# Seven block products in place of eight in the second layer of a two-layer decoder trunk

## The chip, the cores and the metric

The kernel runs on one core of one Trainium2 chip, in one launch. The metric is the device time of a run in microseconds (us); the host only lays arrays out before and after. Three runs of the kernel before took 833.39, 834.37 and 834.68 us.

## What is computed

One inference step of a trunk of two layers, over 512 prompt positions and 8 sample positions that share all parameters: 520 positions of 1024 channels, in float32. The first layer (two convolutions behind an input projection of 7168 columns, then an output projection) is computed as before. The second layer is:

```python
def c_mixer(x, w_in, w_s, b_s, norm_v_g, norm_v_b, w_out):
    z = jnp.einsum('bld,de->ble', x, w_in)             # 1024 -> 3 x 2048
    u, v, g = jnp.split(z, (D_C, 2 * D_C), axis=-1)
    u = jax.nn.gelu(u)
    v = layer_norm(jax.nn.gelu(v), norm_v_g, norm_v_b)  # over all 2048 channels
    ...
    w_causal = w_s * jnp.tril(jnp.ones((CHUNK, CHUNK), w_s.dtype))
    mix = jnp.einsum('hts,bnshd->bnthd', w_causal, vc) + jnp.transpose(b_s)[None, None, :, :, None]
    mix = mix.reshape(bsz, n_chunks * CHUNK, D_C)[:, :seq]
    y = u * mix * jax.nn.silu(g)
    return jnp.einsum('ble,ed->bld', y, w_out), v
```

`vc` is v in chunks of 128 positions and 8 groups of 256 channels. Each layer ends in `x = layer_norm(alpha * x + mixer(x))`.

## The kernel before

**Layout.** Channels lie on the 128 partitions, the 520 positions along the free axis in two halves of 260 (`TH`), since one half fits a bank of PSUM. A product is exact to float32 by splitting both sides into a high and a low part in the type fp32r: per slice of 128 input channels and per half, three matmuls, high by high, low by high, high by low. A **unit** is 128 output channels of 1024 inputs: 8 slices x 2 halves x 3 = 48 matmuls of 260 columns. `mm2` (L154 to L168) issues a unit with both halves side by side, `mm` (L142) one half; `zt` takes a z tile of two banks from the PSUM pool `zps`, which has two such buffers, `cps` has two single banks, `mps` two for transposes and mixes.

**Weights.** `load_unit` (L116) takes a unit's 512 KB from DRAM on SyncE's DMA queue (`raw`, three buffers), has ScalarE cast the high part (`whi`, L121), and VectorE subtract the low part (`wlo`, L128); for units 10 to 49 ScalarE writes the negated weight (L125) and GpSimd's queue adds the weight onto it by an accumulating DMA (L126). Twelve slots hold high and low parts; `unit(n)` keeps five units loaded ahead.

**Order.** The engines run in order. The order on each is fixed when the program is built, by a scheduler that walks the code with a model of time and with the priorities that `soon()` (earlier) and `background()` (later) set.

**Second layer.** x1 is the first layer's result (`res`), split into `x1h` and `x1l`.

1. Sixteen v units. The first six go by halves (L630 to L641), ten by `mm2` (L642 to L647). Each gets a gelu on ScalarE and then `v_tok` (L616): four transposes on TensorE to put positions on the partitions, a copy out by ScalarE (L622) into `vtok`, four statistics on VectorE (L624). All sixteen `vtok` stay in SBUF.
2. `v_finish` (L655): mean and variance per position, and 64 normalisations of 128x128 on VectorE (L663), in place; also the row sums of w_s and the samples' part.
3. `c_group(g0)` (L733), four times. Each does four u units with a gelu (L741), then the four gate units with a silu (L756); for each gate VectorE forms u·gate (L757), `mix_unit` (L710) does four mixing matmuls with `vtok` (L718), and `split_y` (L400) multiplies by the mix and splits y into high (ScalarE, L406) and low (VectorE). Gelu and silu need different function tables on ScalarE: a table load stands where one follows the other, so twice a group.
4. After two groups, eight output units `z_q` (L773) over the first 1024 channels of y, put into `r1`; after the other two, `out_part` (L482), the second half of the output projection with the final norm.

Of the kernel before, what the change touches and what calls it, by code (L numbers as in the profile page):

```python
# [20 lines left out]
NS = 8  # L21
# [20 lines left out]

LEAD = 5
CUT = 260
NWARM = 28
POOL_MUL = (3, 7)
# [4 lines left out]
def decoder_kernel(  # L51
# [45 lines left out]
    def zt(name):  # L97
        return zps.tile([P, 2, 512], F32, tag="z", name=name)
# [13 lines left out]

    n_units = 2 + wu.shape[0]
    units = [None, None]

    def load_unit(wtag=("W", 12)):  # L116
        n = len(units)
        raw = wpool.tile([P, KT, P], F32, tag="raw", name=f"raw_{n}", bufs=3)
        nc.sync.dma_start(raw, wu[n - 2])
        hi = wpool.tile([P, KT, P], F32R, tag=wtag[0], name=f"whi_{n}", bufs=wtag[1])  # L120
        nc.scalar.copy(hi, raw)  # L121
        lo = wpool.tile([P, KT, P], F32R, tag=wtag[0], name=f"wlo_{n}", bufs=wtag[1])
        if n in BY_DMA:

            nc.scalar.mul(lo, raw, -1.0)  # L125
            nc.gpsimd.dma_start(lo, wu[n - 2], accum_op=ALU.add)  # L126
        else:
            nc.vector.tensor_tensor(lo, raw, hi.bitcast(F32), op=ALU.subtract)  # L128
# [12 lines left out]

# [146 lines left out]
    for i in range(KT):  # L288
# [70 lines left out]
    with background():  # L359
        for j in range(2):  # L360
            nc.gpsimd.dma_start(cas_out[:, 4 * j : 4 * j + 4], xs[j])
            proda = wpool.tile([P, 4, NS, WA], F32, tag="M", name=f"proda_{j}", bufs=4)
            nc.vector.tensor_tensor(
                proda,
                xs[j],
                pa[:, 4 * j : 4 * j + 4, None, PA_W : PA_W + WA].to_broadcast([P, 4, NS, WA]),
                op=ALU.mult,
            )
            cas = tiny.tile([P, 4, NS], F32, name=f"cas_{j}")
            nc.vector.tensor_reduce(cas, proda, axis=AX.X, op=ALU.add)  # L370
            for i in range(4 * j, 4 * j + 4):
                nc.scalar.activation(
                    cA[i][:, SEQ:], cas[:, i - 4 * j, :], AF.Identity, bias=pa[:, i, PA_B : PA_B + 1]
                )
# [83 lines left out]
    for d in range(KT):  # L458
        xr = tmp(f"xr_{d}")
        nc.sync.dma_start(xr, xT[:, d, :])  # L460
        r = slots.tile([P, T], F32, tag="SB", name=f"r_{d}", bufs=8)
# [12 lines left out]
        res.append(r)  # L474
# [138 lines left out]
    vs = tiny.tile([P, NV, NS], F32, name="vs")  # L613
    stats = wpool.tile([P, NC, NV, 6], F32, tag="M", name="stats", bufs=4)

    def v_tok(i):  # L616
        nc.gpsimd.tensor_copy(vs[:, i, :], vt[i][:, SEQ:])
        m = mt(f"vt_{i}")
        for c in range(NC):
            nc.tensor.transpose(m[:, c * P : (c + 1) * P], vt[i][:, c * P : (c + 1) * P], ident)  # L620
        t = ab_slot(f"vtok_{i}") if i < 8 else slots.tile([P, T], F32, tag="SB", name=f"vtok_{i}", bufs=8)
        nc.scalar.copy(t[:, :SEQ], m)  # L622
        for c in range(NC):
            nc.vector.bn_stats(stats[:, c, i, :], t[:, c * P : (c + 1) * P])  # L624
        vtok[i] = t

# [6 lines left out]
    for i in range(NVF):  # L633
# [6 lines left out]
        if i > 0:  # L640
            v_tok(i - 1)  # L641
    for i in range(NVF, NV):  # L642
        z = zt(f"z_v{i}")
        mm2(halves(z), unit(n + i), x1h, x1l)
        vt[i] = y_slot(F32, f"v_{i}")
        nc.scalar.activation(two(vt[i]), zh(z), AF.Gelu_apprx_tanh)
        v_tok(i - 1)  # L647
    n += NV

    mv = tiny.tile([P, NC, 2], F32, name="mv")  # L650
    rs = tiny.tile([P, NC], F32, name="rs")
    mixs = tiny.tile([P, NV, NS], F32, name="mixs")
    rowsum = wpool.tile([P, NH, P], F32, tag="M", name="rowsum", bufs=4)

    def v_finish():  # L655
        v_tok(NV - 1)
# [3 lines left out]
        nc.gpsimd.tensor_tensor(rs, rs, neg_half[:, :NC], op=ALU.pow)  # L660
        for i in range(NV):
            for c in range(NC):
                nc.vector.tensor_scalar(  # L663
                    vtok[i][:, c * P : (c + 1) * P],
                    vtok[i][:, c * P : (c + 1) * P],
                    mv[:, c, 0:1],
                    rs[:, c : c + 1],
                    op0=ALU.subtract,
                    op1=ALU.mult,
                )  # L670

# [37 lines left out]

    def mix_unit(i):  # L710
        h = i // 2
# [5 lines left out]
        for c in range(NC):  # L717
            nc.tensor.matmul(  # L718
                m[:, c * P : (c + 1) * P], vtok[i][:, c * P : (c + 1) * P], wt[:, h, :], start=True, stop=True
            )  # L720
# [11 lines left out]

    def c_group(g0):  # L733
        nonlocal n
        gu = []
        for i in range(g0, g0 + 4):
            z = zt(f"z_u{i}")
            mm2(halves(z), unit(n), x1h, x1l)
            n += 1
            t = btmp(f"gu_{i}")  # L740
            nc.scalar.activation(two(t), zh(z), AF.Gelu_apprx_tanh)  # L741
            gu.append(t)
            if i == 0:
                v_finish()

        def finish(i):
            t = gu[i - g0]
            split_y(i, t, mix_unit(i), "c", 1)

        for i in range(g0, g0 + 4):  # L750
            z = zt(f"z_gc{i}")
            mm2(halves(z), unit(n), x1h, x1l)
            n += 1
            g = tmp(f"silu_c{i}")
            t = gu[i - g0]
            nc.scalar.activation(two(g), zh(z), AF.Silu)  # L756
            nc.vector.tensor_tensor(t, g, t, op=ALU.mult)  # L757
            if g0 > 0:
                finish(i)
        if g0 == 0:  # L760
            for i in range(4):
                finish(i)
# [129 lines left out]
```

## Time and profile before

| | us |
|---|---|
| median of three runs | 834.37 |
| profiled execution, time | 834.73 |
| profiled execution, span from the first to the last instruction | 833.0 |
| mean granted TensorE clock, share of full | 0.990 |
| VectorE, ScalarE, GpSimd busy (share of the span) | 536.6 (64%), 347.2 (42%), 88.0 (11%) |
| share of the DMA queues of SyncE and GpSimd of 16 engines | 32.2%, 15.0% |

PE is TensorE's matmuls and PEld its weight loads, DVE is VectorE, ACT ScalarE, POOL GpSimd, SP SyncE; a q behind a name is that engine's instruction queue. A group row gives line, engine, operation, output <- inputs with shape and type, xcount, then busy time in us and mean ns of one, then the engine's idle time just before these instructions with what ended most of it. A row of the chain of waits gives start, duration, engine and work, in us. A row of windows gives the stretch in us, then seven or more entries in the order PE, PEld, DVE, ACT, POOL: the busy time with the count of instructions, then the mean granted clock, the DMA share and GB/s.

### The profile page before, as it was taken

Reading aid. Unit: us, or ns where it says so; the run is one execution under the profiler, and the core shown is the slowest. Engines: PE = TensorE matmul, PEld = TensorE weight load, DVE = VectorE, ACT = ScalarE, POOL = GpSimd, SP = SyncE. Lnnn points to the kernel's source line nnn. Section 1 sums busy time; section 2 is a strip of 40 time slices with the busy share of each in tenths; the row PEclk is TensorE's granted clock in tenths of the full one; section 3 lists DMA queues with packets and bytes.
Section 4 is the critical chain, followed back from the end, with each engine's and each line's share of the span. In section 5 each row is a group of like instructions: output and inputs, shape, how many; then the busy total and the mean of one; then the engine's idle time right before and its main releaser. Section 6 shows DMA issues by size and latency. Waiting matters only on the chain.

```text
span 833.0 us, 16028 instructions
## 1 busy us (share of the span) xinstructions
PE 814.2 (98%) x6792; PEld 812.2 (98%) x6792; DVE 536.6 (64%) x914; ACT 347.2 (42%) x510; POOL 88.0 (11%) x158
## 2 busy tenths in 40 slices
PE   8999999999999999999989999999999999999994
PEld 8999999999999999999979999999999999999993
DVE  5899998999962576446885432596355433526566
ACT  5545454455354444442647423323432133334243
POOL 0121221221110000000021111100000000000032
PEclk9999999999999999999989999999999999999997
DMA  8798988889888543231331432214233223222011
GB/s 290 208 206 191 209 185 185 184 191 216 182 173 189 167 115 102 79 124 52 84 119 51 128 85 93 77 56 126 78 87 92 84 94 102 77 87 92 1 53 52
DMA packets 32873, 103.37 MB, mean 124 GB/s; under 512 B 4209, under 2 KB 7937, under 8 KB 32801
## 3 DMA queue, kind: packets, MB, share of 16 engines
q1 hardware_dynamic: 26000, 79.01, 32.2%
q0 software_dynamic: 6800, 23.33, 15.0%
q8 instruction: 53, 0.87, 0.4%
q14 instruction: 20, 0.16, 0.1%
HBM read 98.89 MB, written 3.44 MB: 123 GB/s over the span
## 4 chain that ended last, share of the span: by engine, by line
PE 96%; DMA 1%; DVE 1%; ACT 0%; SPq 0%; issue 0%; ACTq 0%; DVEq 0%
PE z_p L146 11%; PE z_gc L162 11%; PE z_u L162 11%; PE z_v L162 7%; PE z_q L162 6%; PE z_o L162 6%; PE z_c L162 5%; PE z_ga L162 5%; PE z_post L162 5%; PE z_h L162 5%; PE z_gb L162 5%; PE z_val L162 5%; PE z_gate L162 5%; PE z_v L146 5%; PE mix L718 2%; PE vt L620 1%
## 5 line engine op out<-in xcount | busy, mean ns | idle before, releaser
L121 ACT CAST whi<-raw 128x1024 fp32r<-128x1024 f32 x134 | 139.9, 1048 | 324.9 <-PE z_u L162 44.9
L128 DVE TENSOR_TENSOR wlo<-raw,whi 128x1024 fp32r<-128x1024 f32 x94 | 114.4, 1224 | 142.5 <-ACT whi L121 141.9
L274 DVE SCALAR_TENSOR_TENSOR acc<-apad,pa,acc 128x512 f32<-128x512 f32 x240 | 165.7, 751 | 3.6 <-ACT acc L271 2.7
L162 PE MATMUL z_gc<-x1h,whi 128*128 128x260 f32 x256 | 72.9, 285 | 0.0
L162 PE MATMUL z_u<-x1h,whi 128*128 128x260 f32 x256 | 72.4, 283 | 0.0
L162 PE MATMUL z_gc<-x1h,wlo 128*128 128x260 f32 x256 | 72.0, 281 | 0.0
L162 PE MATMUL z_u<-x1l,whi 128*128 128x260 f32 x256 | 72.0, 281 | 0.0
L162 PE MATMUL z_gc<-x1l,whi 128*128 128x260 f32 x256 | 72.0, 281 | 0.0
L162 PE MATMUL z_u<-x1h,wlo 128*128 128x260 f32 x256 | 72.0, 281 | 0.0
L126 POOL DMA_DIRECT2D wlo<-in_wu x40 | 34.7, 869 | 139.2 <-ACT wlo L125 132.2
L162 PEld LDWEIGHTS z_u<-x1h,wlo 128*128 128x128 f32 x256 | 48.1, 188 | 0.1
L162 PEld LDWEIGHTS z_gc<-x1h,wlo 128*128 128x128 f32 x256 | 48.2, 188 | 0.0
L162 PEld LDWEIGHTS z_gc<-x1l,whi 128*128 128x128 f32 x256 | 48.1, 188 | 0.0
L162 PEld LDWEIGHTS z_u<-x1h,whi 128*128 128x128 f32 x256 | 48.0, 188 | 0.1
L162 PEld LDWEIGHTS z_u<-x1l,whi 128*128 128x128 f32 x256 | 48.1, 188 | 0.0
L162 PEld LDWEIGHTS z_gc<-x1h,whi 128*128 128x128 f32 x256 | 48.1, 188 | 0.0
L162 PE MATMUL z_v<-x1h,whi 128*128 128x260 f32 x160 | 46.0, 287 | 0.0
L162 PE MATMUL z_v<-x1h,wlo 128*128 128x260 f32 x160 | 45.0, 281 | 0.0
L162 PE MATMUL z_v<-x1l,whi 128*128 128x260 f32 x160 | 45.0, 281 | 0.0
L125 ACT ACTIVATE wlo<-raw 128x1024 fp32r<-128x1024 f32 x40 | 42.2, 1055 | 0.0
L162 PE MATMUL z_c<-xh,wlo 128*128 128x260 f32 x128 | 36.1, 282 | 0.3 <-DVE wlo L128 0.3
L146 PE MATMUL z_p<-yh_c,whi 128*128 128x260 f32 x128 | 36.3, 284 | 0.0
(260 smaller groups left out, 2723.4 us busy)
## 6 DMA issues: line engine op xcount, KB each, us to landing
raw<-in_wu SPq DMA_DIRECT2D x134, 512.0 KB, 3.9
wlo<-in_wu POOLq DMA_DIRECT2D x40, 512.0 KB, 7.7
xr<-in_xT SPq DMA_DIRECT2D x8, 260.0 KB, 4.2
x<-in_xT SPq DMA_DIRECT2D x7, 260.0 KB, 5.1
out_y<-r SPq DMA_DIRECT2D x8, 130.0 KB, 1.7
out_y<-out SPq DMA_DIRECT2D x4, 260.0 KB, 2.2
raw_s<-in_w SPq DMA_DIRECT2D x8, 128.0 KB, 4.5
xs<-in_cache_a SPq DMA_DIRECT2D x2, 496.0 KB, 8.2
```

Of the source, the lines that this page charges most:

```text
L121: nc.scalar.copy(hi, raw)
L125: nc.scalar.mul(lo, raw, -1.0)
L126: nc.gpsimd.dma_start(lo, wu[n - 2], accum_op=ALU.add)
L128: nc.vector.tensor_tensor(lo, raw, hi.bitcast(F32), op=ALU.subtract)
L146: nc.tensor.matmul(ps, a[:, k, :], b[k][:, c], start=(k == 0 and j == 0), stop=(k == KT - 1 and j == 2),)
L162: nc.tensor.matmul(z[h][:, :TH], a[:, k, :], b[k][:, hs(h)], start=(k == 0 and j == 0), stop=(k == KT - 1 and j == 2),)
L274: nc.vector.scalar_tensor_tensor(acc[i], apads[i][:, j : j + SEQ], pa[:, i, PA_W + j : PA_W + j + 1], acc[i], op0=ALU.mult, op1=ALU.add,)
L620: nc.tensor.transpose(m[:, c * P : (c + 1) * P], vt[i][:, c * P : (c + 1) * P], ident)
L718: nc.tensor.matmul(m[:, c * P : (c + 1) * P], vtok[i][:, c * P : (c + 1) * P], wt[:, h, :], start=True, stop=True)
```

## The change

**Block products.** Two units with the same inputs, (W1, W2), are taken as a 2x2 matrix of blocks: two units by two halves of 512 input channels; x1 likewise: two halves of the channels by two halves of the positions. Such a product of 2x2 blocks can be had with seven products of blocks in place of eight. One product is 4 slices x 3 = 12 matmuls of 260 columns; a pair takes 84 where two units take 96. Pairs are ten v units (6 to 15, five pairs) and twelve of the sixteen (u unit, gate unit) **items**; items 3, 7, 11 and 15 (`PLAIN`) stay two units each.

**What that needs.** Sums of weight blocks (`load_pair`): four sums on VectorE (s1 to s4, 128x512), five high parts on ScalarE (`ws1` to `ws4`, `wa22`, L153) and five low parts on VectorE, beside high and low of W1. Sums of x1's blocks, once (`x_forms`): 16 sums on VectorE, 16 high parts and 16 low parts. Sums of the results (`Seven`): a z tile and one bank of `cps` collect them, three copies out by ScalarE and three additions by VectorE with a PSUM operand.

**What it moves.** An item now runs through at once, so that its gelu (L910) and its two silu (L911 reads PSUM, L912 the SBUF half) stand together, after the *next* item's first product (`step`); weights are asked for by jobs, ten slots ahead (`need`). v goes to DRAM from `v_tok`, and comes back for one item at a time (`fetch`) on SyncE's queue; its normalisation, four activations with scale and bias (L869), is ScalarE's. `r1` goes to DRAM and back as well. In the second layer W1's low part of a pair, and both of a plain item, come by the accumulating DMA.

```diff
-LEAD = 5
+WSLOTS = 12
+AHEAD = 10
+PLAIN = (3, 7, 11, 15)
...
+    def load_pair(n1, n2):
+        r1 = load_raw(n1)
+        hi, lo = parts(n1, r1)
+        r2 = load_raw(n2)
...
+        def split(h, low, src):
+            nc.scalar.copy(h, src)
+            nc.vector.tensor_tensor(low, src, h.bitcast(F32), op=ALU.subtract)
...
+        a11, a12, a21, a22 = r1[:, :4], r1[:, 4:], r2[:, :4], r2[:, 4:]
+        s1 = add("s1", a21, a22)
+        s2 = add("s2", s1[2], a11)
+        split(*s1)
+        s4 = add("s4", s2[2], a12)
+        split(*s2)
+        s3 = add("s3", a11, a21)
+        split(*s3)
+        split(*form("a22"), a22)
+        split(*s4)
...
+    def need(*job):
+        j = place[job]
+        ahead = lambda: sum(2 if len(q) == 1 else 7 for q in JOBS[j + 1 : len(loaded)])
+        while len(loaded) < len(JOBS) and (len(loaded) <= j or ahead() < AHEAD):
...
-        t = ab_slot(f"vtok_{i}") if i < 8 else slots.tile([P, T], F32, tag="SB", name=f"vtok_{i}", bufs=8)
-        nc.scalar.copy(t[:, :SEQ], m)
+        t = tmp(f"vtok_{i}")[:, :SEQ]
+        nc.scalar.copy(t, m)
         for c in range(NC):
             nc.vector.bn_stats(stats[:, c, i, :], t[:, c * P : (c + 1) * P])
-        vtok[i] = t
+        vtok[i] = spill.tile([P, SEQ], F32, name=f"vd_{i}")
+        nc.gpsimd.dma_start(vtok[i], t)
...
+        def head(self):
+            (hi, lo), self.w = need(*self.job)
...
+            product(self.b1, self.a1(0), self.x(0, 0), True)
+            with soon():
+                nc.scalar.copy(self.s12[:, hs(0)], self.b1)
+
+        def body(self):
+            product(self.b2, self.s("s1"), self.f(1), True)
+            product(self.b1, self.s("s2"), self.f(2))
+            with soon():
+                nc.scalar.copy(self.s12[:, hs(1)], self.b1)
+            b3 = cps.tile([P, SEQ], F32, tag="cv", name=f"z_{self.key}_2")[:, :TH]
+            product(b3, self.a1(1), self.x(1, 0), True)
+            with soon():
+                nc.vector.tensor_tensor(self.c1[:, hs(0)], self.s12[:, hs(0)], b3, op=ALU.add)
+            product(self.b1, self.s("s3"), self.f(3))
+            with soon():
+                nc.scalar.copy(self.s3, self.b1)
+                nc.vector.tensor_tensor(self.c22, self.s3, self.b2, op=ALU.add)
+
+        def tail(self):
+            product(self.b1, self.s("a22"), self.f(4))
+            product(self.b2, self.s("s4"), self.x(1, 1))
+            with soon():
+                nc.vector.tensor_tensor(
+                    self.c1[:, hs(1)], self.s12[:, hs(1)], self.b2, op=ALU.add
+                )
+            return self.b1
...
+    def step(p, end):
+        p.head()
+        if flight[0] is not None:
+            flight[0]()
+        p.body()
+        flight[0] = end
...
-        for i in range(NV):
-            for c in range(NC):
-                nc.vector.tensor_scalar(
...
+        nc.vector.scalar_tensor_tensor(nmr, mv[:, :, 0], -1.0, rs, op0=ALU.mult, op1=ALU.mult)
...
+    def fetch(i):
+        t = tmp(f"vback_{i}")[:, :SEQ]
+        nc.sync.dma_start(t, vtok[i])
+        for c in range(NC):
+            nc.scalar.activation(
...
+    def gate_end(p, i, g):
+        z = p.tail()
+        nc.scalar.activation(p.c1, p.c1, AF.Gelu_apprx_tanh)
+        nc.scalar.activation(g[:, hs(0)], z, AF.Silu, scale=-1.0)
+        nc.scalar.activation(g[:, hs(1)], p.c22, AF.Silu, scale=-1.0)
+        finish(i, p.c1, g)
...
+        t = spill.tile([P, T], F32, name=f"rd_{d}")
+        nc.gpsimd.dma_start(t, r)
...
+        r = r_slot(f"r2_{d}")
+        nc.sync.dma_start(r, r1[d])
```

**Order on ScalarE, items 8 to 10.** Before, the gate part of the third group, from the table load at its first silu:

```order
L756 ACT_TABLE_LOAD
L756 ACTIVATE silu_c8_8196<-z_gc8_8141 128x520
L406 CAST yh_c8_8209<-gu_8_7968 128x520
L121 CAST whi_123_8290<-raw_123_8288 128x1024
L756 ACTIVATE silu_c9_8269<-z_gc9_8214 128x520
L406 CAST yh_c9_8282<-gu_9_8025 128x520
L121 CAST whi_124_8363<-raw_124_8361 128x1024
L756 ACTIVATE silu_c10_8342<-z_gc10_8287 128x520
```

Now, from behind item 8's silu of PSUM (with the copy `s3_c9` and the cast `whi_119` left out between), up to item 9's silu of PSUM, `g_9<-z_c9`, which is the last reader of item 9's z tile:

```order
L912 ACTIVATE g_9_8351<-g_9_8351 128x260
L473 CAST yh_c8_8421<-u_8_8241 128x520
L131 ACTIVATE wlo_119_8363<-raw_119_8359 128x1024
L746 COPY s12_c10_8520<-z_c10_8519 128x260
L127 CAST whi_120_8489<-raw_120_8487 128x1024
L869 ACTIVATE vback_9_8479<-vback_9_8479,nmr_6472,rs_6471 128x128 x4
L131 ACTIVATE wlo_120_8491<-raw_120_8487 128x1024
L153 CAST ws1_120_8498<-s1_120_8496 128x512
L910 ACT_TABLE_LOAD
L910 ACTIVATE u_9_8350<-u_9_8350 128x520
L911 ACT_TABLE_LOAD
L911 ACTIVATE g_9_8351<-z_c9_8366 128x260
```

Between two silu stood one cast and the next gate's weight; now stand there the next pair's weights, a fetched v and two table loads, and g_9's SBUF half (L912) goes ahead of the gelu, in the silu table of item 8.

**Order on TensorE at the same place.** Before, a gate unit, four mixes of the last item, the next gate unit (`vtok_9` lies in SBUF from the v units on):

```order
L162 MATMUL z_gc9_8214<-x1l_7_4859,whi_117_7916 128x260
L718 MATMUL mix_9_8274<-wt_5169,vtok_9_5943 128x128 x4
L162 MATMUL z_gc10_8287<-x1h_0_4816,whi_118_7973 128x260
L162 MATMUL z_gc10_8287<-x1h_0_4816,wlo_118_7975 128x260
L162 MATMUL z_gc10_8287<-x1l_0_4817,whi_118_7973 128x260
```

Now, the end of item 10's product with `ws2` and the beginning of plain item 11's u unit; ahead of these rows stand, 12 each, item 10's first product, item 9's with `wa22` and `ws4`, and item 10's with `ws1`:

```order
L721 MATMUL z_c10_8519<-xf1_2_5570,ws2_114_8257 128x260
L886 MATMUL mix_9_8566<-wt_5171,vback_9_8479 128x128
L721 MATMUL z_c10_8519<-xf1_2_5570,ws2_114_8257 128x260 x2
L886 MATMUL mix_9_8566<-wt_5171,vback_9_8479 128x128
L721 MATMUL z_c10_8519<-xf1_3_5629,ws2_114_8257 128x260
L886 MATMUL mix_9_8566<-wt_5171,vback_9_8479 128x128
L721 MATMUL z_c10_8519<-xf1_3_5629,ws2_114_8257 128x260 x2
L886 MATMUL mix_9_8566<-wt_5171,vback_9_8479 128x128
L721 MATMUL z_c12_2_8913<-x1h_4_4842,whi_120_8489 128x260
L229 MATMUL z_u11_8640<-x1h_0_4818,whi_115_8354 128x260
L229 MATMUL z_u11_8640<-x1h_0_4818,wlo_115_8356 128x260
L229 MATMUL z_u11_8640<-x1l_0_4819,whi_115_8354 128x260
```

The z tiles of items 9, 10 and 11 share the two buffers of `zps`, so `z_u11` takes the buffer of `z_c9`, which the silu at the end of the ScalarE piece reads last. From the first matmul of item 10, which takes the buffer of `z_c8`, to the first of `z_u11` stand 61 matmuls of 260 columns and four mixes; before, a z tile and the one that follows it on the other buffer were a whole unit of 48 each.

More of the change, by code (lines that the diff above doesn't have):

```diff
@@ L132, in decoder_kernel @@
     BY_DMA = set(range(10, 50))
-    EXTRA = set()
+    EXTRA = {}
     for base in (64, 128):
-        EXTRA.update((base + 6, base + 7))
+        EXTRA[base + 6] = ("M", "M")
+        EXTRA[base + 7] = ("M", "raw")
+    JOBS = [(n,) for n in range(2, 78)]
+    JOBS += [(n, n + 1) for n in range(78, 88, 2)]
+    for half in range(2):
+        base = 88 + 24 * half
+        for i in range(8):
+            m = base + i // 4 * 8 + i % 4
+            if 8 * half + i in PLAIN:
+                JOBS += [(m,), (m + 4,)]
+                BY_DMA.update((m, m + 4))
+            else:
+                JOBS += [(m, m + 4)]
+                BY_DMA.add(m)
+        JOBS += [(n,) for n in range(base + 16, base + 24)]
@@ L137, in unit @@
+    place = {job: j for j, job in enumerate(JOBS)}
+    loaded = []
+    def need(*job):
+        j = place[job]
+        ahead = lambda: sum(2 if len(q) == 1 else 7 for q in JOBS[j + 1 : len(loaded)])
+        while len(loaded) < len(JOBS) and (len(loaded) <= j or ahead() < AHEAD):
+            q = JOBS[len(loaded)]
+            loaded.append(load_unit(*q) if len(q) == 1 else load_pair(*q))
+        return loaded[j]
     def unit(n):
-        while len(units) < min(n + 1 + LEAD, n_units):
-            load_unit(("M", 4) if len(units) in EXTRA else ("W", 12))
@@ L140, in unit @@
-        return units[n]
+        return need(n)
     def mm(ps, w, ah, al, c):
@@ L218, in decoder_kernel @@
                     )
-    load_unit()
+    loaded.append(load_unit(2))
     pa = const.tile([P, KT, NPA], F32, name="pa")
@@ L234, in decoder_kernel @@
     nc.gpsimd.memset(neg_half, -0.5)
-    unit(1)
+    loaded.extend(load_unit(m) for m in range(3, 7))
     xs = []
     for j in range(2):
-        t = wpool.tile([P, 4, NS, WA], F32, tag="M", name=f"xs_{j}", bufs=4)
+        t = wpool.tile([P, 4, NS, WA], F32, tag="M", name=f"xs_{j}", bufs=3)
         nc.sync.dma_start(t, cache_a[:, 4 * j : 4 * j + 4])
@@ L332, in decoder_kernel @@
         nc.gpsimd.dma_start(cbp_out[:, i, :], ch[:, SEQ : SEQ + PADB])
-        s = slots.tile([P, T], F32, tag="SB", name=f"sB_{i}", bufs=8)
+        s = r_slot(f"sB_{i}")
         sB.append(s)
@@ L460, in decoder_kernel @@
         nc.sync.dma_start(xr, xT[:, d, :])
-        r = slots.tile([P, T], F32, tag="SB", name=f"r_{d}", bufs=8)
+        r = r_slot(f"r_{d}")
         if d == 2:
@@ new lines, in product, with __init__ @@
+    def product(ps, a, b, first=False):
+        for k in range(4):
+            (ah, al), (bh, bl) = a(k), b(k)
+            for j, (p, q) in enumerate(((ah, bh), (al, bh), (ah, bl))):
+                nc.tensor.matmul(
+                    ps, p, q, start=(first and k == 0 and j == 0), stop=(k == 3 and j == 2),
+                    skip_group_check=True,
+                )
+    class Seven:
+        def __init__(self, key, job, c1, c22):
+            self.key, self.job, self.c1, self.c22 = key, job, c1, c22
+        def head(self):
+            (hi, lo), self.w = need(*self.job)
+            self.a1 = lambda half: lambda k: (hi[:, 4 * half + k], lo[:, 4 * half + k])
+            self.x = lambda half, h: lambda k: (
+                x1h[4 * half + k][:, hs(h)],
+                x1l[4 * half + k][:, hs(h)],
+            )
+            self.f = lambda j: lambda k: (xf[j - 1][k][:, 0], xf[j - 1][k][:, 1])
+            self.s = lambda name: lambda k: (self.w[name][:, 0, k], self.w[name][:, 1, k])
+            z = zt(f"z_{self.key}")
+            self.b1, self.b2 = z[:, 0, :TH], z[:, 1, :TH]
+            self.s12, self.s3 = btmp(f"s12_{self.key}"), btmp(f"s3_{self.key}")[:, :TH]
+            product(self.b1, self.a1(0), self.x(0, 0), True)
[20 more added lines that the diff above has]
+                    self.c1[:, hs(1)], self.s12[:, hs(1)], self.b2, op=ALU.add
+                )
+            return self.b1
@@ L641, in decoder_kernel, with v_end @@
             v_tok(i - 1)
[L642 to L647, printed above, removed]
+        if i < 4:
+            x_forms(i)
+    v_tok(NVF - 1)
+    flight = [None]
+    def v_end(p, i):
+        z = p.tail()
+        nc.scalar.activation(vt[i], p.c1, AF.Gelu_apprx_tanh)
+        nc.scalar.activation(vt[i + 1][:, hs(0)], z, AF.Gelu_apprx_tanh, scale=-1.0)
+        nc.scalar.activation(vt[i + 1][:, hs(1)], p.c22, AF.Gelu_apprx_tanh, scale=-1.0)
+        v_tok(i)
+        v_tok(i + 1)
+    def step(p, end):
[4 more added lines that the diff above has]
+        flight[0] = end
+    for i in range(NVF, NV, 2):
+        vt[i], vt[i + 1] = y_slot(F32, f"v_{i}"), y_slot(F32, f"v_{i + 1}")
+        p = Seven(f"v{i}", (n + i, n + i + 1), vt[i], vt[i + 1][:, hs(1)])
+        step(p, lambda p=p, i=i: v_end(p, i))
     n += NV
@@ L731, in mix_unit @@
         return t
[L733 to L743, printed above, removed]
-                v_finish()
[L746 to L762, printed above, removed]
+    back = {}
@@ new lines, in finish, with c_half @@
+    def finish(i, u, g):
+        nc.vector.tensor_tensor(u, u, g, op=ALU.mult)
+        split_y(i, u, mix_unit(i, back[i]), "c", 1)
+    def gate_end(p, i, g):
+        z = p.tail()
+        nc.scalar.activation(p.c1, p.c1, AF.Gelu_apprx_tanh)
+        nc.scalar.activation(g[:, hs(0)], z, AF.Silu, scale=-1.0)
+        nc.scalar.activation(g[:, hs(1)], p.c22, AF.Silu, scale=-1.0)
+        finish(i, p.c1, g)
+    def c_half(half):
+        base = 88 + 24 * half
+        for i in range(8):
+            e = 8 * half + i
+            m = base + i // 4 * 8 + i % 4
+            u, g = tmp(f"u_{e}"), tmp(f"g_{e}")
+            if e in PLAIN:
+                z = zt(f"z_u{e}")
+                mm2(halves(z), unit(m), x1h, x1l)
+                if flight[0] is not None:
+                    flight[0]()
+                    flight[0] = None
+                nc.scalar.activation(two(u), zh(z), AF.Gelu_apprx_tanh)
+                z = zt(f"z_gc{e}")
+                mm2(halves(z), unit(m + 4), x1h, x1l)
+                nc.scalar.activation(two(g), zh(z), AF.Silu)
+                back[e] = fetch(e)
+                finish(e, u, g)
+                continue
+            p = Seven(f"c{e}", (m, m + 4), u, g[:, hs(1)])
+            step(p, lambda p=p, e=e, g=g: gate_end(p, e, g))
+            if e == 0:
+                v_finish()
+            back[e] = fetch(e)
```

101 lines of the change are left out of this document (65 added, 36 removed).

## The prediction

> **What bounds the kernel now.** I read the page's shares first, then the chain of work that ended last, the waits, and the windows of the (u, gate) stage.
>
> ```profile
> PE 814.2 (98%) x6792; PEld 812.2 (98%) x6792; DVE 536.6 (64%) x914; ACT 347.2 (42%) x510; POOL 88.0 (11%) x158
> PE 96%; DMA 1%; DVE 1%; ACT 0%; SPq 0%; issue 0%; ACTq 0%; DVEq 0%
> PE z_v L146 <- DVE r L492: 4.1, 1, 4.1
> ```
>
> TensorE is the chain: 96% of the span, with one wait above 1.2 us. In the second layer it never waits:
>
> ```profile
> 673.25 22.85 PE z_u L162 x192
> 696.10 5.70 PE z_gc L162 x48
> 702.69 5.73 PE z_gc L162 x48
> 673.00:722.00 49.00, 49.00 (x416) 49.00 (x415) 19.73 (x25) 16.96 (x21) 0.75 (x3) 1.00 0.29 88
> 722.00:772.00 50.00, 50.00 (x424) 50.00 (x423) 21.80 (x28) 19.49 (x25) 0.50 (x2) 1.00 0.28 85
> ```
>
> The first three rows are of the chain: 192 matmuls take 22.85 us, 0.119 us each (the 0.28 us of one matmul in the groups is latency). From 696.10 to 702.69 pass 6.59 us for a unit of 48 and a mix, so a mix costs 0.89 us. The last two are windows over a group of four items each, an item being one u unit with its gate: PE busy throughout, ScalarE (fourth time) 17 to 19.5 of 49 to 50 us, mean clock 1.00, DMA share 0.29. ScalarE and VectorE have slack, and every matmul taken away is 0.119 us gained as long as they keep up.
>
> **The gain.** A pair in seven products issues 7 x 12 = 84 matmuls where two units issued 96; the order shows 12 to a product and nothing else new on TensorE. Five v pairs and twelve items make 17 x 12 x 0.119 = **24.3 us**. A group of four (three in seven products, one plain) goes from 384 matmuls and four mixes (49.2 us) to 348 and four (45.0).
>
> **What is put on ScalarE in that group.** Rows, by form:
>
> ```profile
> L121 ACT CAST whi<-raw 128x1024 fp32r<-128x1024 f32 x134 | 139.9, 1048 | 324.9 <-PE z_u L162 44.9 <-PE z_v L162 41.6 <-PE z_q L162 34.4
> L125 ACT ACTIVATE wlo<-raw 128x1024 fp32r<-128x1024 f32 x40 | 42.2, 1055 | 0.0
> L567 ACT ACTIVATE r<-r,pa 128x260 f32<-128x260 f32 x24 | 13.0, 598 | 5.8 <-DVE r L566 5.8
> L372 ACT ACTIVATE cA<-cas,pa 128x8 f32<-128x8 f32 x8 | 2.0, 288 | 0.0
> L446 ACT ACTIVATE cA<-cA,pa 128x520 f32<-128x520 f32 x8 | 5.9, 814 | 0.0
> L406 ACT CAST yh_c<-gu 128x520 fp32r<-128x520 f32 x16 | 10.0, 626 | 34.8 <-DVE gu L405 34.8
> L741 ACT ACTIVATE gu<-z_u 128x520 f32<-128x520 f32 x16 | 9.6, 602 | 9.4 <-PE z_u L162 9.4
> L632 ACT COPY v<-z_v 128x260 f32<-128x260 f32 x6 | 2.2, 370 | 2.2 <-PE z_v L146 2.2
> L638 ACT ACTIVATE v<-v 128x260 f32<-128x260 f32 x6 | 2.1, 410 | 0.0
> L756 ACT ACT_TABLE_LOAD x4 | 5.1, 1283 | 0.1
> ```
>
> Five whi at 1.05 and five negated copies for the DMA at 1.06: 10.5. Fifteen casts of a 128x512 form: no row, between 0.41 (260 wide) and 0.63 (520), taken at 0.62: 9.3. Nine copies out of PSUM at 0.37: 3.3. Sixteen 128-wide normalisations of fetched v with a scale and a bias pointer: no row, between 0.29 (8 wide) and 0.60 (260 wide, two pointers); on the slope of the 260 and 520 rows (0.83 ns an element) 0.49: 7.8. Four gelu, silu (six of 260, one of 520) and four yh: 7.9. Table loads: two an item, eight a group, where a group had two: 10.3. Sum **49.1 us** busy, against 18. Instructions in a row overlap a little:
>
> ```profile
> 696.02 1.05 ACT L121 CAST whi<-raw 128x1024 fp32r<-128x1024 f32 x1 [4.15 <-PE z_u L162]
> 696.97 0.60 ACT L741 ACTIVATE gu<-z_u 128x520 f32<-128x520 f32 x1
> 701.72 1.04 ACT L121 CAST whi<-raw 128x1024 fp32r<-128x1024 f32 x1 [4.15 <-PE z_gc L162]
> 702.78 1.28 ACT L756 ACT_TABLE_LOAD   x1
> 704.08 0.61 ACT L756 ACTIVATE silu_c<-z_gc 128x520 f32<-128x520 f32 x1
> ```
>
> The gelu starts 0.95 us after a cast of 1.05, so 0.1 comes off each of some 57; a table load neither overlaps nor drains, 1.30 from start to start. That leaves about 43.5 us in 45.0 of TensorE: **97%**, on an engine that runs in order and waits in its turn for weight slots, VectorE and DMAs.
>
> [...]
>
> **Where it reaches TensorE.** Two PSUM buffers hold z. An item's buffer comes free with its last silu (L911), which stands behind two table loads, and the item after next needs it. Take the pieces of order shown with the change. From z_c8's release to z_c9's, ScalarE has s3 0.37, whi 1.05, silu 0.41, yh 0.63, wlo 1.06, s12 0.37, whi 1.05, four normalisations 1.96, wlo 1.06, ws1 0.62, load 1.28, gelu 0.63, load 1.28, silu 0.38: 12.15, less some 1.25 overlap, 10.9 us. TensorE has 61 matmuls and a mix before z_u11 wants that buffer: 8.1. It waits **2.8**. Going on, release of z_c9 to release of z_c10 holds 12.2 us of ScalarE work plus 2.3 in which the cast of yh_c9 waits for VectorE (u·g, mix, u·mix, at these rows):
>
> ```profile
> L757 DVE TENSOR_TENSOR gu<-silu_c,gu 128x520 f32<-128x520 f32 x16 | 11.2, 699 | 0.3
> L722 DVE SCALAR_TENSOR_TENSOR mix<-mix,pv,cm 128x512 f32<-128x512 f32 x16 | 12.0, 751 | 29.2 <-PE mix L718 29.2
> ```
>
> Against 96 matmuls and a mix, 12.3: **2.2** more. z_c10's head, by the same walk, comes 1.5 late behind c8's normalisations and loads. A group's waits: 6.5 to 7. Walking the other three I get 7.5 (with the statistics of v ahead), 9 and 5; the last two include 1.9 each for a weight whose low part comes by DMA:
>
> ```profile
> wlo<-in_wu POOLq DMA_DIRECT2D x40, 512.0 KB, 7.7
> raw<-in_wu SPq DMA_DIRECT2D x134, 512.0 KB, 3.9
> ```
>
> (its ScalarE copy ends about 6 us before b3 of c6 and of c14 asks for it). Four groups at 7 = **28 us**. Bounds: 0 a group if everything is hidden, 10 if each release comes an extra us late.
>
> **The v pairs.** VectorE has a wlo, nine ops on 512, three sums out of PSUM and eight statistics:
>
> ```profile
> L128 DVE TENSOR_TENSOR wlo<-raw,whi 128x1024 fp32r<-128x1024 f32 x94 | 114.4, 1224 | 142.5 <-ACT whi L121 141.9
> L492 DVE TENSOR_TENSOR r<-z_p,r 128x260 f32<-128x260 f32 x32 | 13.1, 425 | 12.0 <-PE z_p L146 12.0
> L624 DVE BATCH_NORM_STATS2 stats<-vtok 128x6 f32<-128x128 f32 x64 | 13.9, 280 | 1.0 <-ACT vtok L622 1.0
> L663 DVE TENSOR_SCALAR vtok<-vtok,mv,rs 128x128 f32<-128x128 f32 x64 | 16.5, 363 | 0.4 <-POOL rs L660 0.4
> ```
>
> 1.22 + 9 x 0.69 (512 wide has no two-input row of its own; the 520 row is 0.70) + 3 x 0.43 + 8 x 0.28 = 11.0, about 9.5 with overlap, in 84 matmuls and two units of transposes, 10.0 + 1.8 = 11.8 us; no table load stands there. The 16 sums and 16 low parts of x cost VectorE 32 x 0.43 = 13.7 spread over the six plain v units. I take 1.5 us of waits in all, between 0 and 5. The 64 normalisations of L663 leave VectorE: not on the path, nothing gained. Spilling v and the half sums adds some 12 MB at a DMA share of 0.29: nothing, while a fetch is asked for a unit ahead.
>
> **Sum.** Against the profiled execution's 834.7 (span 833.0; 0.4 above the median): 834.7 - 24.3 + 28 + 1.5 = **840 us**.
>
> **Rivals.**
> 1. *ScalarE keeps step; faster.* At 0 to 4.5 us of waits a group the time is 812 to 829. For it: 43.5 is still under 45.0, and the three items without switches could be caught up in. Against it: the interval above, 10.9 against 8.1, has no slack to borrow from. It decides at 5.7 a group, where the waits eat the gain; were the two loads free, the interval would be 8.3 and rival 1 would be right.
> 2. *The clock drops.* One wait in the trace shows what a longer one does:
>
> ```profile
> 420.00:425.00 5.00, 0.85 (x6) 0.61 (x5) 4.86 (x14) 1.79 (x5) 2.56 (x3) 0.91 0.71 281
> 425.00:428.00 3.00, 3.00 (x15) 3.00 (x16) 3.00 (x6) 1.29 (x4) 2.51 (x3) 0.50 0.00 0
> 424.83 7.07 PE z_v L146 x34
> ```
>
> After 4.1 us of idling the clock is 0.50 and 34 matmuls take 7.07 us instead of 4.05: 3.0 lost. My waits are 1.5 to 3.2, just short of it. If one a group passes that point, +12: 852; with two, 860. [...]
> 3. *A switch also drains.* If each load kept ScalarE as long again, 1.3 more, a group would need 43.5 + 8 x 1.3 = 54 us there: 9 over TensorE's 45, and with the waits above 16 a group, 834.7 - 24.3 + 64 + 1.5 = 876. The rows show 1.30 from start to start. [...]
>
> That the change doesn't do what it says is excluded by the order (84 matmuls to a pair).
>
> **How the numbers follow.** Forecast, 5.5 to 9 us of waits a group, 833 to 848: 0.50. Rival 1: 0.37. Rival 2: 0.10. Rival 3: 0.03. A measurement here tells 0.2% (1.7 us) from no change. The same, 0.07, is the forecast's lower edge; faster is rival 1, 0.37; slower the rest, 0.56. These lie on both sides: the forecast's own range is 833 to 848; the range for 8 in 10 takes in rival 1's upper part and rival 2's single drop, 821 to 852.
>
> **What would show it.** A matmul every 0.119 us and 84 a pair; 33 table loads in the (u, gate) stage for 7; ScalarE at 80% or more of each group's window; TensorE waiting for L911 ahead of the heads of every third item, of z_u and of z_gc, 1.5 to 3 us each; groups of about 52 us for 49; v pairs with their transposes in about 12 us, where two v units took 2 x 5.71 + 2 x 0.89 = 13.2. Wrong if the groups come to 47 or less (rival 1), if PEclk falls under 9 there (rival 2), or if TensorE's waits name another engine than ScalarE.

## The result, and the profile after

The changed kernel takes 873.47 us against 834.16: a ratio of 1.047 (95% interval 1.044 to 1.049), slower by 39 us, outside the range of 821 to 852. The profiled spans are 871.7 and 833.0 us. In experiment 5 below, one of four runs was slow (1265.16 us at a mean clock of 0.583), and its time is the median of the other three. From the page after, the busy shares and the chain that ended last:

```profile
PE 811.5 (93%) x6588; PEld 803.2 (92%) x6588; DVE 601.9 (69%) x1050; ACT 478.3 (55%) x772; POOL 121.4 (14%) x202
PE 72%; ACT 10%; DVE 7%; DMA 6%; issue 4%; POOL 1%; SPq 0%; ACTq 0%; DVEq 0%; POOLq 0%
```

204 matmuls are gone (17 pairs x 12), as counted. But TensorE is 72% of the chain in place of 96%, and ScalarE 10%. The waits of TensorE that this document counts, longest in total first (us in total, times, the longest):

```profile
PE z_gc L229 <- ACT g L911: 10.5, 4, 3.3
PE z_c L721 <- ACT g L911: 7.8, 4, 2.3
PE z_u L229 <- ACT g L911: 6.6, 3, 2.7
PE z_v L213 <- DVE r L559: 3.1, 1, 3.1
PE z_c L721 <- DVE u L756: 2.7, 2, 1.3
PE z_c L721 <- DMA wlo<-in_wu: 2.3, 1, 2.3
PE z_c L721 <- ACT s_c L746: 2.2, 3, 0.7
PE z_p L213 <- ACT yh_c L473: 2.1, 1, 2.1
PE z_v L721 <- ACT s_v L746: 1.8, 2, 1.1
PE st L451 <- ACT parts_col L449: 1.4, 1, 1.4
PE z_v L721 <- DVE wlo L134: 1.2, 1, 1.2
PE z_gb L229 <- ACT silu_b L489: 1.1, 1, 1.1
PE z_v L721 <- DVE xf L714: 1.0, 1, 1.0
PE z_v L721 <- ACT s_v L752: 0.6, 1, 0.6
PE z_c L721 <- ACT whi L127: 0.4, 1, 0.4
```

The first three are the forecast's: a z tile that the silu of L911 releases, at heads, z_u and z_gc. ScalarE ahead of one of them, by time:

```profile
612.18 1.06 ACT L131 ACTIVATE wlo<-raw 128x1024 fp32r<-128x1024 f32 x1 [0.39 <-PE z_c L721]
613.26 1.28 ACT L910 ACT_TABLE_LOAD   x1
614.55 0.64 ACT L910 ACTIVATE u<-u 128x520 f32<-128x520 f32 x1
615.19 1.28 ACT L911 ACT_TABLE_LOAD   x1
616.49 0.39 ACT L911 ACTIVATE g<-z_c 128x260 f32<-128x260 f32 x1
```

The silu ends at 616.88; the head that waits for it starts at 616.93, 2.2 us late. A load starts 0.02 us behind the end of what stands ahead of it (613.24 to 613.26) and 1.29 us before what follows it, so these rows show no drain. The operations without a row of their own cost what was interpolated (a normalisation of 128 columns 0.486 us for 0.49, the 512-wide cast 0.618 for 0.62):

```profile
L153 ACT CAST ws<-s 128x512 fp32r<-128x512 f32 x48 | 29.4, 618 | 40.5 <-PE z_q L229 17.2 <-PE z_gc L229 10.2 <-DVE s L158 9.6
L869 ACT ACTIVATE vback<-vback,nmr,rs 128x128 f32<-128x128 f32 x64 | 26.5, 486 | 0.8 <-DMA vback<-vd 0.8
```

Windows over the second and the third group (the fourth busy time is ScalarE's):

```profile
593.03:648.22 55.19, 46.54 (x370) 45.55 (x369) 29.75 (x48) 42.78 (x68) 3.86 (x7) 0.97 0.57 153
695.86:753.48 57.62, 50.08 (x387) 49.28 (x386) 30.93 (x53) 41.08 (x66) 6.09 (x10) 0.94 0.59 149
```

ScalarE has about the work that was forecast (43.5 us), but in groups of 55 and 58 us, so it is busy 78% and 71% of them, where 97% was forecast.

What the forecast did not have is the clock. Windows of TensorE around four waits, cut at multiples of 3.413 us from one another (to 0.1), the length of one of its stretches at half clock (first PE's busy time, in the last three entries the granted clock, DMA share and GB/s):

```profile
555.48:558.89 3.41, 1.22 (x10) 1.22 (x11) 1.94 (x7) 3.33 (x5) 0.06 (x1) 1.00 0.88 240
558.89:562.30 3.41, 3.41 (x18) 3.41 (x17) 1.87 (x6) 2.58 (x4) 1.42 (x4) 0.50 0.78 157
582.72:586.14 3.42, 0.49 (x4) 0.49 (x5) 1.74 (x3) 3.38 (x5) 0.02 (x1) 1.00 0.94 153
586.14:589.55 3.41, 3.41 (x19) 3.41 (x18) 1.76 (x4) 1.88 (x3) 0.00 (x0) 0.50 0.00 0
640.81:644.22 3.41, 1.86 (x15) 1.86 (x16) 2.05 (x4) 3.37 (x5) 0.00 (x0) 1.00 0.78 281
801.24:804.65 3.41, 1.70 (x15) 1.49 (x14) 1.00 (x2) 3.38 (x5) 0.23 (x1) 1.00 0.54 174
804.65:808.07 3.42, 3.42 (x29) 3.42 (x30) 3.03 (x4) 3.08 (x4) 0.00 (x0) 1.00 0.29 109
```

The windows with 1.22 and 0.49 us of work are followed by a window at half clock, the one with 1.70 by full clock. The wait of 2.25 us at 555.4 lies in one window and costs the next its clock; the one of 2.45 us at 639.9 lies across an edge and costs nothing. In such a stretch 15 or 16 matmuls start, some 0.22 us from start to start for 0.119, so it loses about 1.6. The second layer has seven such stretches, 11 us, beside the one at its beginning, which the kernel before has too, and one more lies in the first layer.

That last one is in z_gb, which takes 51.0 us for 45.9. ScalarE's first operation of the last three-tap convolution, sB_7, stands at 191.41 before; after, it stands behind the last accumulators of the long convolution:

```profile
191.41 0.71 ACT L335 ACTIVATE sB<-ch,pa 128x512 f32<-128x512 f32 x1
```

```profile
238.16 0.69 ACT L350 ACTIVATE cA<-acc,pa 128x512 f32<-128x512 f32 x1 [0.93 <-DVE acc L341]
238.75 0.71 ACT L402 ACTIVATE sB<-ch,pa 128x512 f32<-128x512 f32 x1
```

So z_post7's tile is read late, and TensorE waits 1.4 and 1.1 us in z_gb.

### The profile page after: what moved, and what is told of

It reads as the page before. It is cut to its first block, busy times and chain, and to the rows that moved or that the text cites. A ratio compares the mean times of both kernels' runs of the same rounds, so it can differ in the third digit from the quotient of the medians.

```text
span 871.7 us, 16301 instructions
## 1 busy us (share of the span) xinstructions
PE 811.5 (93%) x6588; PEld 803.2 (92%) x6588; DVE 601.9 (69%) x1050; ACT 478.3 (55%) x772; POOL 121.4 (14%) x202
## 4 chain that ended last, share of the span: by engine, by line
PE 72%; ACT 10%; DVE 7%; DMA 6%; issue 4%; POOL 1%; SPq 0%; ACTq 0%; DVEq 0%; POOLq 0%
PE z_p L213 8%; PE z_c L721 7%; PE z_gb L229 5%; PE z_q L229 5%; PE z_o L229 5%; PE z_c L229 5%; PE z_ga L229 5%; PE z_post L229 5%; PE z_h L229 5%; PE z_val L229 5%; PE z_gate L229 5%; DMA raw<-in_wu 4%; PE z_v L213 4%; PE z_gc L229 3%; PE z_u L229 2%
## 5 line engine op out<-in xcount | busy, mean ns | idle before, releaser
L134 DVE TENSOR_TENSOR wlo<-raw,whi 128x1024 fp32r<-128x1024 f32 x57 | 69.5, 1223 | 66.3 <-ACT whi L127 65.8
L153 ACT CAST ws<-s 128x512 fp32r<-128x512 f32 x68 | 41.7, 619 | 50.0 <-DVE s L158 19.1
L721 PE MATMUL z_c<-xf,ws 128*128 128x260 f32 x432 | 61.0, 291 | 2.2 <-ACT s_c L746 2.2
L154 DVE TENSOR_TENSOR ws<-s,ws 128x512 fp32r<-128x512 f32 x68 | 45.9, 685 | 24.2 <-ACT ws L153 23.7
L721 PEld LDWEIGHTS z_c<-xf,ws 128*128 128x128 f32 x432 | 55.7, 193 | 3.0 <-ACT s_c L746 2.9
L229 PE MATMUL z_gb<-xh,whi 128*128 128x260 f32 x128 | 36.9, 288 | 1.1 <-ACT silu_b L489 1.1
L229 PE MATMUL z_q<-yh_c,whi 128*128 128x260 f32 x128 | 36.5, 286 | 0.3 <-DVE r L947 0.3
L213 PE MATMUL z_p<-yh_c,wlo 128*128 128x260 f32 x128 | 36.8, 288 | 0.0
L229 PE MATMUL z_gb<-xh,wlo 128*128 128x260 f32 x128 | 36.7, 287 | 0.0
L229 PE MATMUL z_gb<-xl,whi 128*128 128x260 f32 x128 | 36.6, 286 | 0.0
```

Of the source, the lines that this page charges most:

```text
L153: nc.scalar.copy(h, src)
L154: nc.vector.tensor_tensor(low, src, h.bitcast(F32), op=ALU.subtract)
L213: nc.tensor.matmul(ps, a[:, k, :], b[k][:, c], start=(k == 0 and j == 0), stop=(k == KT - 1 and j == 2),)
L229: nc.tensor.matmul(z[h][:, :TH], a[:, k, :], b[k][:, hs(h)], start=(k == 0 and j == 0), stop=(k == KT - 1 and j == 2),)
L721: nc.tensor.matmul(ps, p, q, start=(first and k == 0 and j == 0), stop=(k == 3 and j == 2), skip_group_check=True,)
```

## The experiments

Theory A: z comes free late, behind two table loads, and the waits it makes also lower the clock. Rival B: ScalarE is simply full. C: the first layer's order. D: what makes the clock drop. All times are against the kernel before, measured beside each (833.2 to 834.2); a ratio with its interval is given where a verdict rests on it. In the expectations e1 to e8 are experiments 1 to 8, and e10, e12, e11 and e13 are 9, 10, 11 and 12.

**1. The gate block copied out at once.**

```diff
+        with soon():
+            nc.vector.tensor_copy(g[:, hs(0)], z)
         nc.scalar.activation(p.c1, p.c1, AF.Gelu_apprx_tanh)
-        nc.scalar.activation(g[:, hs(0)], z, AF.Silu, scale=-1.0)
-        nc.scalar.activation(g[:, hs(1)], p.c22, AF.Silu, scale=-1.0)
+        nc.scalar.activation(g, g, AF.Silu, scale=-1.0)
```

> The twelve items' gate block in PSUM is copied to SBUF by VectorE at once, and one silu of 520 reads SBUF; the z buffer no longer waits for the two table loads, which all stay. Theory A (late release of z behind the loads sets TensorE's waits, and these waits pull the clock down): the waits for L911, 24.9 us, go, with some 6 of 8 clock drops at 2.0 us and the refill of 11 waits at 0.16: 873.5 less 25 to 39, 835 to 848. Rival B (ScalarE, at 43.5 of 45 us a group, is simply full): the waits come back at casts and copies, gain under 10, 863 or more.

845.99 us: 27.5 below the changed kernel. No wait for the silu is left, and of seven clock drops two are. Of the 33 loads of the stage 27 stay, against the expectation: with one silu an item the order on ScalarE came out with six fewer. These loads and the shorter silu take 7.7 and 2.0 us off ScalarE. The largest waits in the stage now, at most 2.1 us at a time:

```profile
PE z_c L721 <- DVE g L760: 5.2, 3, 2.1
PE z_c L721 <- ACT s_c L746: 3.4, 4, 1.1
```

A holds, by its own sum; B had 863 or more, and 9.7 us less on ScalarE are too few for 27.5.

**2. No switch of tables.** The gate's `AF.Silu` is `AF.Gelu_apprx_tanh`.

> The gate's silu is replaced by the gelu of the u part, so no function table is switched in the (u, gate) stage and the gate's function is another; order, copies and z's readers stay. Theory A: release to release falls from 10.9 to about 8.3 us against 8.1 of TensorE, so nearly all waits for L911 and their clock drops go: 838 to 848. If the waits are set by VectorE's chain or the DMAs and not by the loads: under 10 us gained, 863 or more. If a switch cost more than the load's 1.28 (a drain), the gain exceeds 40.

836.46 us, 37 below, a little under A's range and short of what a drain would give. This kernel's result is not the trunk's, since its gate is another function. Of the 24.9 us of waits for L911 one row is left:

```profile
PE z_gc L229 <- ACT g L911: 1.3, 3, 0.6
```

Two cures, one with 27 of the stage's loads and one with none, both release z early, and both take the waits away. The second alone would not tell A from B, since it also takes 42 us of loads off ScalarE.

**3. The statistics of norm_a held back.** `mean_of`'s matmuls for `col_stats` are issued after the last of z_gb.

> The two pairs of statistics matmuls (L451, L452) of the first layer's norm_a are held behind the last z_gb matmul, as they stood before; all else as in the changed kernel. Theory C (the scheduler's new place for them, inside z_gb, costs two waits and a clock drop): z_gb takes 45.9 us again for 51.0, 873.5 less 5.1 = 868.4. Rival: the wait only moves to where they stand now, 873.

871.84 us: the rival; the 1.6 us less lie within the spread of the changed kernel's runs (870.7 to 874.5). The two waits are one, at the same place:

```profile
PE z_gb L231 <- ACT silu_b L492: 3.2, 1, 3.2
```

The matmuls' new place was a sign, not the cause, and the late sB_7 was found by following that silu back on ScalarE.

**4. All items plain.** `PLAIN = tuple(range(16))`, and `v_finish()` is called behind item 0's gelu, where before the pair's step called it.

> All 16 items plain (two units of 48 each), with everything else of the change: five v pairs in seven products, items one after the other with two table loads each, v out and back. Theory A: a plain item has 12.3 us of TensorE for some 10.3 of ScalarE, so z comes free in time: 834.7 - 7.1 (five pairs) + 5.1 (first layer) + about 6 (waits of the v pairs) = 836 to 842. Rival B (one item at a time, table loads and the way over DRAM cost by themselves): 850 or more.

848.33 us, neither. The (u, gate) stage is as A says: from 545 to 639 us TensorE is busy 93.0 of 94. The v pairs are dearer than I had them, busy 64.5 of 75, with two clock drops:

```profile
470.00:545.00 75.00, 64.51 (x500) 62.68 (x499) 46.36 (x115) 46.28 (x84) 21.70 (x29) 0.95 0.63 182
545.00:639.00 94.00, 92.96 (x777) 92.38 (x776) 34.17 (x66) 66.04 (x90) 13.84 (x22) 1.00 0.70 168
```

So the change is 25 us slower with the twelve pairs of the stage than without them, though they save 17.1 us of matmuls.

**5. Two tags for the one of 16 slots.**

```diff
-        return slots.tile(list(shape), dt, tag="R", name=name, bufs=16)
+        return slots.tile(list(shape), dt, tag=tag, name=name, bufs=8)
...
-        s = r_slot(f"sB_{i}")
+        s = r_slot(f"sB_{i}", tag="R2")
```

> The one pool tag R of 16 slots is two tags of 8 again (cA and half of the sums of x1 in one, sB, r and the other half in the other); all else as in the changed kernel. Theory C2 (in one tag sB_7 waits for its turn behind cA_7, whose accumulators end late; its three-tap conv moves from 191 to 239 us, z_post7's buffer and the silu of z_gb0 come late, and TensorE waits twice in z_gb, with a clock drop): z_gb takes 45.9 us for 51.0, 868.4. Holding the statistics alone gave back 1.6; if the order of layer 1 doesn't matter: 872 to 874.

867.9 us, about as said. In the first layer sB_7 stands early again, at 190.46, and no wait and no clock drop is left in z_gb, which takes 45.9 us again. The shared tag is the cause; that it is the order of allocation in it was argued from where sB_7 stands.

**6. Idle matmuls in the waits.**

```diff
+    def filler():
+        m = mt("fill")
+        for j in range(NFILL):
+            with tc.issue_after(last[0]):
+                last[1] = nc.tensor.matmul(
+                    m[:, :TH], x1h[0][:, :P], x1h[1][:, :TH], start=True, stop=True
+                ).ins
```

> Twelve idle matmuls of 260 columns (nobody reads their result) ahead of each place in the (u, gate) stage where TensorE waits for L911 (heads of items 2, 6, 10, 14; z_u and z_gc of the plain items): 144 more matmuls, 17.1 us of work. Theory D (a wait that fills over half of a clock window of 3.41 us halves the clock for the next window, 2.0 us each, six or seven times): the silu end when they did, the filling lies in the waits, at most 1.9 us of idling is left, the drops in the groups go: 858 to 867. If the drops have nothing to do with idling: 873 or more. If the filling adds up: 880 to 890.

872.24 us, with 17 us more of work on TensorE: half a result. From item 1 on, the windows at half clock go from six to three, two of them in a row, and the clock over 550 to 650 us from 0.95 to 0.98. But the time didn't fall: a wait for L911 is replaced by one for a copy that ScalarE makes for the next product, which itself now comes later.

```profile
PE z_c L724 <- ACT s_c L769: 9.6, 4, 3.4
```

The drop in the first layer is gone too, though nothing was changed there. Its two waits are as long as before, 1.4 and 1.1 us, but they lie otherwise in the windows. First the changed kernel's window, with half clock behind it, then this run's, with full clock behind it:

```profile
241.43:244.84 3.41, 1.33 (x6) 0.96 (x7) 1.65 (x3) 3.38 (x5) 0.00 (x0) 1.00 0.75 148
```

```profile
239.58:242.99 3.41, 1.98 (x13) 1.45 (x12) 2.08 (x4) 2.19 (x3) 0.00 (x0) 1.00 0.86 202
```

The drops follow the idling within a window (D), at 1.6 us each and not 2.0. A border at half a window, as the expectation has it, is not shown (the last section has 1.55 us with full clock behind it and 1.94 with half). But TensorE and ScalarE wait for each other, so the end of a wait is not fixed, as I had assumed.

**7 and 8. One load an item; then low parts by VectorE.** Items in turn gelu-silu and silu-gelu, with edits 1 and 5; in the second, `BY_DMA.add(m)` for pairs is taken out as well.

> Three edits together: the gate block copied out by VectorE (as in e1), two tags (as in e5), and items taken in turn gelu-silu and silu-gelu (a plain odd item's gate unit goes ahead of its u unit), so that a table is loaded once an item and not twice: 26 loads for 41. Theory A with B as the rest (after e1, what waits is left comes from a full ScalarE): 846 - 5.1 - a third to a half of the 16 us of waits that e1 kept in the stage and its drop: 831 to 838. If ScalarE's load no longer matters: 841. Faster than before needs under 832.5.

> As e7, and the low part of a pair's first u unit is VectorE's again (1.22 us) in place of ScalarE's negated copy (1.06) and GpSimd's accumulating DMA (7.5 to land): 12.7 us less on ScalarE and 14.7 more on VectorE over the stage; the waits for a low part by DMA (1.8 at item 0, 1.9 at items 6 and 14 in the forecast) go. If ScalarE sets the rest: 1 to 4 below e7. If VectorE's chain (sums, low parts, u and gate) does: above e7.

841.97 and 849.99 us. By their sum, edits 1 and 5 alone would be at about 841: with z freed, fewer loads (26 in all, for 35 in experiment 1) brought nothing net. Whether they gained something that a new wait then cost is not shown. The low parts on VectorE, with which the order came out with 30 loads, cost 8. Both have a new largest wait, for v that comes back from DRAM; in the first, with two windows at half clock in it and behind it:

```profile
PE mix L886 <- ACT vback L869: 6.6, 2, 5.0
```

**9 to 11. Gelu and tanh.** The gate's silu as x/2 (1 + tanh(x/2)), with edits 1 and 5.

```diff
-        nc.scalar.activation(g, g, AF.Silu, scale=-1.0)
+        nc.scalar.activation(p.s12, g, AF.Tanh, scale=-0.5)
+        nc.vector.scalar_tensor_tensor(g, p.s12, 1.0, g, op0=ALU.add, op1=ALU.mult)
```

In the first and the third, `back[e] = fetch(e)` stands ahead of the item's step; in the third the v units are plain.

> The gate block copied out by VectorE (e1), two tags (e5), an item's v asked for ahead of its head and not behind its weights, and the gate's silu taken as x/2 (1 + tanh(x/2)): tanh on ScalarE, one more VectorE operation of 520 (0.75 us) for an item. Gelu and tanh are in one table, so 33 loads of the stage go and the result stays. Theory A: e2, which left the switches out, gave 836.5; less 5 for the first layer, less some 2 for its waits for L911: 828 to 833, faster than the kernel before from 832.5 down. Rival: VectorE's 12 us more and its chain (e8) take the gain, 836 or more.

> As e10, with v asked for behind the item's weights as in the changed kernel. If the queue of weights ahead of an item's v matters (4.96 us of waiting for item 1's v in e7): 3 to 6 above e10. If not: within 1.5 of e10.

> As e10, with all sixteen v units plain, so 60 matmuls, 7.1 us, more. If the v pairs keep what they save less the 5 to 7 us of waits that the trace of the changed kernel shows among them: within 2 of e10. If their waits cost less here: 5 to 7 above e10. If they cost more than they save: below e10.

844.89, 836.17 and 844.27 us. Asking for v earlier made it 8.7 worse, against the expectation. In the first, TensorE waits longest, 7.3 us, for item 2's v, which is issued at 551.02 and takes 12.8 us to land, beside three accumulating DMAs; beside the drop at its beginning, the second layer has five windows at half clock there and one in the second kernel. Why the other waits grew is not shown. That the v pairs save nothing net holds, 844.27 against 844.89. In the second one wait stands out, since item 1's v, issued at 550.85, takes 11.2 us to land among three accumulating DMAs (its wait, and the DMA issues from 540 to 565 us with KB each and the median us to landing):

```profile
PE mix L886 <- ACT vback L869: 6.3, 3, 5.6
```

```profile
wlo<-in_wu POOLq DMA_DIRECT2D x3, 512.0 KB, 9.4
vback<-vd SPq DMA_DIRECT2D x1, 256.0 KB, 11.2
```

**12. Three low parts by VectorE.** `BY_DMA -= {95, 96, 97}` on the second of these.

> As e12_tanh_late, with the low parts of units 95, 96 and 97 by VectorE and not by accumulating DMA, so that at 548 to 561 us three 512 KB accumulations no longer run beside the weights and item 1's v. In e12 that v is issued at 550.85, lands 11.2 us later, and the mixes of item 1 wait 5.59 us, with a clock drop behind them. If the accumulations are what holds the v up: the wait falls under 2 us and the drop goes, 829 to 832, faster than the kernel before. If the weights ahead of it in SyncE's queue do, or VectorE's 3.7 us more come back as a wait: 834 to 837.

828.22 us, just under the range of 829 to 832, a ratio of 0.9925 (0.9911 to 0.9938): **faster than the kernel before**, by 6 us or 0.75%, with an interval that lies clear of 1, and by 45 us than the changed one. The same stretch of DMA:

```profile
wlo<-in_wu POOLq DMA_DIRECT2D x1, 512.0 KB, 8.3
vback<-vd SPq DMA_DIRECT2D x2, 256.0 KB, 3.6
```

The wait for item 1's v and the drop behind it are gone. The largest wait in the stage is 1.8 us, at item 0, and one clock drop is left in the second layer, beside the one at its beginning.

## Why the prediction was wrong

Slower was right, and so was the place. Against the forecast's sum, from the profiled executions:

| term | forecast | measured |
|---|---|---|
| matmuls saved | -24.3 | -24.3 (204 fewer) |
| waits in the groups | 28 | 32.5 (all rows of z_c, z_u, z_gc) |
| waits among the v pairs | 1.5 | 4.6 |
| first layer | 0 | 5.1 |
| clock drops, second layer | 0 | 11.2 (seven of 1.6) |
| last wait, ahead of z_p | 0 | 2.1 |
| wait and drop at the layers' border | 0 | -2.3 (3.1 us of wait for 4.1, 1.6 of drop for 2.9) |
| restarts | 0 | 4.2 (26 waits of 0.16 in the second layer, an estimate) |
| sum | +5.2 | +33.1 |
| span | +5.2 | +38.7 |

A restart is this: a matmul takes 0.28 us to end where 0.119 lie between two, so a wait costs some 0.16 more than its idle time. The last 5.6 us of the 38.7 aren't assigned.

- *Where it reaches TensorE*: right in mechanism, place and size (28 for 32.5); experiments 1 and 2 show it. In the group whose order was walked, 2.8 us at z_u, 2.2 at z_gc and 1.5 at the head of item 10 were forecast; 2.7, 3.0 and 1.1 came.
- *The clock drops* failed. "My waits are 1.5 to 3.2, just short of it" took the one wait in the trace, 4.1 us, for the point from which the clock falls, so the sum put the drops at nothing. Waits of 2.25 us (at 555.4) and 2.21 us (at 614.7), each in one window to 0.04 us, had half clock behind them, so the forecast's own waits bring rival 2 with them, given a chance of 0.10, seven times at about half its price: the drop before lasts two windows, 6.8 us, and each of the seven one. This is the largest missing term, 11.2 of some 33 us. (Two drops a group would have been 840 + 24 = 864 by the prediction's own price, not 860.) Rival 2's sign, PEclk under 9, didn't come: one drop of 3.4 us leaves the mean of a slice of 22 us on the page above 0.9, so that sign could not show it.
- "The order shows 12 to a product and nothing else new on TensorE" failed. Two pairs of statistics matmuls stood 48 matmuls into z_gb and not behind it, and z_gb took 5.1 us more, which comes from a pool tag far away from the block products (experiments 3 and 5).
- *The v pairs*: 4.6 is within the bounds (0 to 5), the value taken was not; with the drops there they give back what they save (experiment 4 and the all-plain v units of 9 to 11).
- *Rival 3*, drained switches at 876, had nearly the measured time, by luck: no run shows its 1.3 us more for each load. A load took 1.28 us, and what followed it started 1.29 us after the load did.
- "Spilling v and the half sums: nothing" held here, with 0.8 us of waiting on ScalarE; in experiments 7 to 11, and only there, the wait for v was TensorE's largest.

## What to carry to other kernels

Copy a PSUM tile out before a function that needs another table, and choose functions that run without a table load between them, as gelu and tanh did here (8 loads for 41): the first gave 27.5 us here; with the second, the tags and three DMAs it was 45. When work is taken from the engine that sets the time, add up waits not only by their length: in the changed kernel each of the nine windows of 3.41 us that waits left with 1.33 us of matmuls or less had half clock behind it, some 1.6 us on top. And read the order of the whole program, also where the diff has only renamed a pool's tag.

## What the runs showed of the hardware

In the changed kernel's trace the drops lie on one grid. Nine stretches at half clock between stretches at full clock are in it, each 3.413 us long, at multiples of 3.413 from one another; the one of the kernel before is 6.827 long. Four of the nine end at 562.28, 589.59, 750.01 and 780.73 us, 8, 47 and 9 times 3.413 apart, whenever the waits ended. Cut from end to end at these distances, the windows of this trace with 0.28 to 1.33 us of matmuls, nine in all, have half clock behind them, and those with 1.70 or more have full clock. A window with 2.71 us in the kernel before, itself at half clock, has half clock behind it (424.13 to 430.96). Over all runs these counts give no sharp border: in experiment 8 a window with 1.55 us had full clock behind it, in experiment 2 one with 1.94 had half:

```profile
519.60:523.01 3.41, 1.55 (x13) 1.34 (x12) 3.41 (x11) 2.46 (x4) 0.10 (x1) 1.00 0.81 240
523.01:526.43 3.42, 3.06 (x23) 2.87 (x24) 2.40 (x5) 1.32 (x4) 0.00 (x0) 1.00 0.70 220
```

```profile
514.55:517.97 3.42, 1.94 (x14) 1.53 (x14) 1.14 (x2) 2.16 (x4) 0.90 (x1) 1.00 0.94 338
517.97:521.38 3.41, 3.41 (x19) 3.41 (x18) 2.99 (x6) 1.57 (x3) 0.23 (x1) 0.50 0.94 208
```

Between gelu by tanh and tanh no table load stood: the four kernels with both (experiments 9 to 12) have 8 loads where the changed kernel has 41. In experiment 9 a gelu of 0.64 us starts at 567.17 and the tanh behind it at 567.72; in the changed kernel a load of 1.28 us stands between gelu and silu (615.19). With three accumulating DMAs of 512 KB beside it, a fetch of 256 KB took 11.2 us to land (the second kernel of 9 to 11, 540 to 565 us); with one, two such fetches took 3.6 (experiment 12, the same stretch). Whether it is the accumulating or only the bytes that slow it was not tried.
